# A fused two-block transformer on one core: context chain held for its conditioning, its weights loaded by SP, compressor loads two ahead, tail squares summed apart

## The chip, the cores and the metric

The kernel runs on one core of one Trainium2 chip. The metric is the device time of the whole program in microseconds (us). All of it is one launch; nothing is computed on the host but a relaying of the weights.

## The reference

The reference runs two blocks one after the other on x (512 tokens of width 1024). Cut to what matters here:

```
x = first_block(x, mem, ...)       # sparse attention + spatial gating, then x + memory_cross_attention(x, mem),
                                   # then x + relu(norm(x) @ w_ff1)^2 @ w_ff2           (d_ff = 4096)
for l in range(2):                 # second block, two layers; xc = ctx (256 tokens) is a second stream
    m  = silu(c)     @ w_mod[l] + b_mod[l]      # 9 rows of 1024: the conditioning of x
    mc = silu(c_ctx) @ w_mod[l] + b_mod[l]      # 9 rows of 1024: the conditioning of the context
    x  = ffn_sublayer(x, m, 0, ...);  xc = ffn_sublayer(xc, mc, 0, ...)
    h  = mod_norm(x, m, 1, ...);      hc = mod_norm(xc, mc, 1, ...)
    # layer 0: both streams are mixed (convolution, pooling, attention) and go through a second ffn_sublayer;
    # layer 1: the context only gives keys and values, kc and vc
return rms_norm_2(x, final_g)
# mod_norm(x, m, i, g) = rms_norm_2(x, g) * (1 + m[3i+1]) + m[3i];   a sublayer's result is gated by m[3i+2]
```

So `w_mod` (2 x 1024 x 9216, float32) is read once, and each of its 9 rows per layer is needed at a fixed place: rows 0 and 1 at a stream's first norm, row 2 at the gate of its first feed-forward part, rows 3 and 4 at its second norm, and so on.

## The kernel before, in words

**Streams and gemms.** x is kept transposed, 8 tiles of 128 x 512; memory and context are 8 tiles of 128 x 256. Products are float32 of high precision: a weight tile `raw` (128 x 1024, 512 KB) is loaded by SP, ScalarE rounds it (`whi`, line 356) and VectorE takes the rest (`wlo`, line 357), in halves; each product is three matmuls, hi by hi, hi by lo, lo by hi (lines 388 to 390 or 416 to 418). One weight tile of a 128-column output is thus 24 matmuls.

**`get`** (line 362) hands out the next weight tile in an order that a first dry pass recorded: it splits tiles up to two ahead (`ensure`), which loads raw tiles up to two further (three raw buffers), and then calls `tick`.

**Conditioning parts.** `tick` (line 565) advances the conditioning by one part (line 580): a tile `wm` (128 x 512, 256 KB, two buffers) is multiplied and summed on VectorE with silu(c), once for each stream that needs it (line 590: the result tile is called `wj` for a first stream and `wm` for the last), each followed by a short read of the sum into `modp`. `load_wm` (line 571) issues the loads, on ScalarE's queue, one part ahead. The plan has 336 parts: 48 for the context's rows 0 to 2 of layer 0, 48 for x's rows 0 to 2, 96 for rows 3 to 8 of both (two sums each), then layer 1. `need_mods` (line 606) runs the parts that are still missing at once, where a row is used.

**The chain of the context.** All work of the context in layer 0 is a generator, `ctx_chain` (line 1375): first norm, feed-forward part, second norm (`norm_c(0, 1)`), keys and values (`kv_c`, 8 weight tiles of 24 matmuls of 256 columns each), mixers, attention. It stands in a queue, and the main stream takes pieces of it where it expects TensorE to wait: `fill(ns)` draws pieces worth so many nominal ns; a piece that yields -1 ends the fill. So the chain runs during the sparse attention (`nsa`), then during the memory attention (line 1227), whose pipeline has 16 units (score product L1253, maximum L1255, exponential L1260, normalisation L1262, transposes L1271 two steps later, and per head a product with the values, L1281). With `norm_c(0, 1)` it asks for rows 3 and 4.

**Norms of x.** The eight squares of a norm are added up tile by tile (`sq_add`, line 451): the first adds on GpSimd, those after tile 3 on VectorE, each one tile late, and the last square is kept apart (`tail`). `col_rstd` (line 470) sums over the partitions with matmuls by ones: 4 blocks of 128 tokens, in each the sum and the tail; then VectorE scales, GpSimd takes the power, TensorE spreads the result over the partitions (L487).

**The compressor** (`compress`, line 906) of the sparse attention loads its own 8 weight tiles `fc` (512 KB) each right before its matmuls; `block1` calls a piece of it after each of the 16 steps of `project_uv`.

Of the kernel before, what the change touches and what calls it, by code (L numbers as in the profile page):

```python
# [206 lines left out]
class Squares:  # L207


    def __init__(self, ap):  # L210
        self.sum, self.tail = ap, None


class Order(list):
# [7 lines left out]
class Body:  # L222
# [137 lines left out]
    def get(self, key, tick=1, ahead=2, kept=False):  # L360
        i = len(self.used)
        self.used.append(key)
        if kept:
            self.used.kept.add(i)
        if self.order is None:
            _, _, nk, nc = self.pk.pieces[key]
            w = self.split_tiles(kept, nk * nc)
            for t in w:
                self.nc.gpsimd.memset(t.bitcast(F32), 0.0)
            self.tick(tick)  # L370
            return [t.rearrange("p (k n) -> p k n", k=nk) for t in w]
        assert self.order[i] == key, (self.order[i], key)
        self.ensure(i + ahead)
        self.tick(tick)
        w = self.split[i]
        self.split[i] = None
        return w
# [71 lines left out]
    def sq_add(self, ss, x, m, late=None, pool=False):  # L449


        if m == 0:
            self.nc.scalar.activation(ss.sum, x, AF.Square)
            return
        t = self.t2(x.shape[-1])
        self.nc.scalar.activation(t, x, AF.Square)
        on_vector = m > 3 and not pool and (late is not None or x.shape[-1] == T)
        add = lambda: (self.nc.vector if on_vector else self.nc.gpsimd).tensor_tensor(ss.sum, ss.sum, t, op=OP.add)
        if late is None or not on_vector:
            return add()  # L460
        if late:
            late.pop()()
        if m == 7:
            ss.tail = t
        else:
            late.append(add)

# [3 lines left out]
    def col_rstd(self, ss, n, dim, slow=False):  # L471

        nb = n // 128
        p = self.aux()
        parts = [ss.sum] + [ss.tail] * (ss.tail is not None)
        for b in range(nb):
            for i, t in enumerate(parts):
                self.nc.tensor.matmul(p[:, b:b + 1], t[:, b * 128:(b + 1) * 128], self.c("ones"), start=i == 0,
                                      stop=i == len(parts) - 1)
        return self.rstd(p[:, :nb], nb, 1.0 / dim, slow)  # L480

    def spread(self, y, nb, p=None, j0=0, step=1):

# [87 lines left out]
    def load_wm(self):  # L571

        while self.wm_loads < min(self.parts + 2, len(self.plan)):
            w = self.wp.tile([128, 512], F32, tag="wm", name="wm", bufs=2)
            l, j, half = self.plan[self.wm_loads][:3]
            self.nc.scalar.dma_start(w, self.d["wmod"][l, j, half])
            self.wms.append(w)
            self.wm_loads += 1

# [66 lines left out]
    def block1(self):  # L646
# [23 lines left out]
        with tc.tile_pool(name="b1", bufs=1) as self.b1:  # L670
            with tc.tile_pool(name="mix1", bufs=1) as mp:
# [33 lines left out]
                for i in range(2):  # L705
# [7 lines left out]
                    for h in range(2):  # L713
                        src = z[64 * h:64 * h + 64].rearrange("p (n t) -> p t n", t=16)
                        for par in range(2):
                            for q in range(2):
                                o = ksp[i][64 * par:64 * par + 64, 8 * q:8 * q + 8, 31 * h:31 * h + 31]
                                s = src[:, par::2, q:q + 31]
                                if par == 0:
                                    nc.scalar.copy(o, s)  # L720
                                else:
                                    nc.vector.tensor_copy(o, s)
                self.project_vg(hh, hl, v2, gates, pair)
                comp = self.compress(ksp, w2, kc, vc, rows, gg)
                memkv = self.mem_kv(mem, mss)
                mh, ml = self.new_h()
                yc = self.keep(2)
# [3 lines left out]
                for n, _ in enumerate(self.project_uv(hh, hl, u, vv, pair)):  # L731
# [8 lines left out]
                        next(memkv)  # L740
                    if n > 7:
                        next(ln, None)
                for g in (comp, ln, pre):
                    self.run(g)
                sg = self.spatial(u, vv, sgw, mh, ml)
# [159 lines left out]

    def compress(self, ksp, w2, kc, vc, rows, gg):
        nc = self.nc
        for i in range(2):
            ps = [self.aux(), self.aux()]
            for q in range(4):  # L910
                w1 = self.fc(F32)
                nc.sync.dma_start(w1, self.d["cw1"][i, q])
                for mt in range(2):
                    for j in range(4):
                        nc.tensor.matmul(ps[mt][:, :63], w1[:, j, mt * 128:(mt + 1) * 128], ksp[i][:, 4 * q + j],
                                         start=q == 0 and j == 0, stop=q == 3 and j == 3)
                yield 1700
            bias = self.small(2)
            ht = self.tc_(64), self.tc_(64)
# [368 lines left out]
    def ffn1(self, hh, hl, ss):  # L1288
        nc, x = self.nc, self.x
        with self.tc.tile_pool(name="ffn1", bufs=2) as fp:  # L1290
# [25 lines left out]
            def dn(g):  # L1316
                gh, gl = G.pop(g)
                late = []
                for mp_ in range(4):
                    w = self.get(("f2", g, mp_))  # L1320
                    for s in range(2):
                        m = 2 * mp_ + s
                        p = self.mm()
# [24 lines left out]
    def ctx_chain(self, y):  # L1348
# [2 lines left out]
        yield from self.norm_c(0, 0, y=y)  # L1351
        yield from self.ffn2(0, 0, False, True)
        self.ffn_ready = True
        yield from self.norm_c(0, 1)
        self.kc, self.vc = self.fc(F32), self.fc(F32)
        yield from self.kv_c(0, self.kc, self.vc)
# [419 lines left out]
    def mix_out(self, l, s, n, x, ss, mh, ml):  # L1776
# [2 lines left out]
        late = None if s else []  # L1779
        for m in range(8):  # L1780
            p = self.mm()[:, :n]
            self.gemm_fm([(p, mh, ml)], self.get((("o", l), m), s == 0))
            nc.vector.scalar_tensor_tensor(x[:, m], p, gate[:, m:m + 1], x[:, m], op0=OP.mult, op1=OP.add)
            self.sq_add(ss, x[:, m], m, late)
            if s == 0:
# [161 lines left out]
```

## Time and profile before

| | us |
|---|---|
| median of 3 runs (3606.37 to 3608.75) | 3607.94 |
| the profiled execution | 3608.67 |
| its span | 3606.9 |
| TensorE busy (PE) | 3363.2, 93% |
| VectorE busy (DVE) | 2045.1, 57% |
| ScalarE busy (ACT) | 1212.0, 34% |
| GpSimd busy (POOL) | 103.3, 3% |
| DMA, mean over the span | 110 GB/s |

PE is the engine to look at: it is busy nearly everywhere, so what matters is the few places where it is not, and which wait ends last there. The profiled execution took 1.8 us more than its span; that much lies around the instructions.

### The profile page before, as it was taken

The numbers are of one execution on the slowest core, as the hardware profiler recorded it, in microseconds if no ns is written. First come the engines' busy times: TensorE is split into PE (matmuls) and PEld (weight loads), VectorE is DVE, ScalarE is ACT, GpSimd is POOL, SyncE is SP. The second block draws the span as 40 slices with busy tenths as digits, with TensorE's granted clock in tenths as the row PEclk, the third lists the DMA queues.
The fourth block names the chain that finished last, engine by engine and source line by source line (L and its number), as shares of the span: only waits on it lengthen the run. The fifth ranks groups of instructions, "written<-read, shape, count | busy, mean of one in ns | idle before, by whom it ended". The sixth has DMA issues, their size and how long they took to land.

```text
span 3606.9 us, 48216 instructions
## 1 busy us (share of the span) xinstructions
PE 3363.2 (93%) x18878; PEld 2935.1 (81%) x18878; DVE 2045.1 (57%) x4231; ACT 1212.0 (34%) x2417; POOL 103.3 (3%) x156
## 2 busy tenths in 40 slices
PE   8969995089999999999999999999999999999999
PEld 7969985068887888788888888888888888878887
DVE  6578665657777766666564444463333454554445
ACT  6335542053333322236542221232122224633222
POOL 1100000010000000000000000010000010000000
PEclk9989997589999999999999999999999999999999
DMA  5444344425443544444333233212212113323332
GB/s 200 168 140 139 119 133 125 136 83 151 147 146 114 154 144 144 130 138 135 107 100 97 91 97 94 74 47 71 65 65 65 60 58 120 99 69 102 98 98 78
DMA packets 143348, 396.79 MB, mean 110 GB/s; under 512 B 16144, under 2 KB 27280, under 8 KB 142608
## 3 DMA queue, kind: packets, MB, share of 16 engines
q1 hardware_dynamic: 94736, 305.61, 26.7%
q10 hardware_dynamic: 48384, 88.10, 8.4%
q8 instruction: 148, 2.42, 0.3%
q14 instruction: 80, 0.66, 0.1%
HBM read 387.36 MB, written 2.10 MB: 108 GB/s over the span
## 4 chain that ended last, share of the span: by engine, by line
PE 83%; DVE 7%; DMA 4%; issue 3%; ACT 3%; POOL 1%; SPq 0%; ACTq 0%; DVEq 0%; POOLq 0%
PE mm L388 19%; PE mm L389 19%; PE mm L390 19%; PE aux L388 5%; PE aux L389 5%; PE aux L390 5%; DMA wm<-in_wmod 3%; DVE wlo L357 1%; PE aux L1748 1%; DVE wm L590 1%; PE mm L416 1%; PE mm L418 1%; PE mm L417 1%; PE mm L401 1%; PE mm L402 1%
## 5 line engine op out<-in xcount | busy, mean ns | idle before, releaser
L357 DVE TENSOR_TENSOR wlo<-raw,whi 128x512 fp32r<-128x512 f32 (+1 forms) x1060 | 692.7, 696 | 452.9 <-ACT whi L356 445.6
L388 PE MATMUL mm<-h,whi 128*128 128x512 f32 (+1 forms) x2352 | 898.3, 382 | 11.1 <-ACT whi L356 10.8
L356 ACT CAST whi<-raw 128x512 fp32r<-128x512 f32 (+1 forms) x1060 | 599.3, 616 | 906.1 <-issue 634.4
L389 PE MATMUL mm<-h,whi 128*128 128x512 f32 (+1 forms) x2352 | 894.3, 380 | 6.4 <-DVE h L512 5.8
L390 PE MATMUL mm<-h,wlo 128*128 128x512 f32 (+1 forms) x2352 | 891.4, 379 | 0.4 <-DVE wlo L357 0.4
L388 PEld LDWEIGHTS mm<-h,whi 128*128 128x128 f32 x2352 | 446.1, 190 | 93.5 <-ACT whi L356 11.0
L389 PEld LDWEIGHTS mm<-h,whi 128*128 128x128 f32 x2352 | 446.2, 190 | 87.7 <-DVE h L512 7.4
L390 PEld LDWEIGHTS mm<-h,wlo 128*128 128x128 f32 x2352 | 445.8, 190 | 83.8 <-DVE wlo L357 0.8
L388 PE MATMUL aux<-h,whi 128*128 128x256 f32 x1056 | 304.1, 288 | 0.7 <-DVE t L509 0.5
L389 PE MATMUL aux<-h,whi 128*128 128x256 f32 x1056 | 301.6, 286 | 0.5 <-DVE h L512 0.3
L390 PE MATMUL aux<-h,wlo 128*128 128x256 f32 x1056 | 301.3, 285 | 0.0
L388 PE MATMUL mm<-g,whi 128*128 128x512 f32 (+1 forms) x720 | 277.9, 386 | 0.0
L389 PE MATMUL mm<-g,whi 128*128 128x512 f32 (+1 forms) x720 | 277.7, 386 | 0.0
L390 PE MATMUL mm<-g,wlo 128*128 128x512 f32 (+1 forms) x720 | 276.7, 384 | 0.0
L590 DVE CUSTOM_DVE_ANT_0 wm<-wm,silu_c 128x512 f32<-128x512 f32 x336 | 232.0, 691 | 67.2 <-DMA wm<-in_wmod 61.0
L1400 DVE SCALAR_TENSOR_TENSOR x<-mm,gate,x 128x512 f32<-128x512 f32 x160 | 120.0, 750 | 180.4 <-PE mm L390 180.3
L388 PEld LDWEIGHTS aux<-h,whi 128*128 128x128 f32 x1056 | 205.0, 194 | 4.9 <-DVE t L509 0.9
L389 PEld LDWEIGHTS aux<-h,whi 128*128 128x128 f32 x1056 | 204.6, 194 | 4.8 <-DVE h L512 1.3
L390 PEld LDWEIGHTS aux<-h,wlo 128*128 128x128 f32 x1056 | 204.6, 194 | 0.0
L421 ACT CAST g<-t 128x512 fp32r<-128x512 f32 x88 | 54.6, 621 | 397.2 <-DVE t L1446 397.2
L1446 DVE SCALAR_TENSOR_TENSOR t<-t,mm 128x512 f32<-128x512 f32 x88 | 60.5, 688 | 212.8 <-PE mm L390 212.4
L390 PEld LDWEIGHTS mm<-g,wlo 128*128 128x128 f32 x720 | 135.3, 188 | 27.5
(364 smaller groups left out, 4898.0 us busy)
## 6 DMA issues: line engine op xcount, KB each, us to landing
raw<-in_w_a SPq DMA_DIRECT2D x220, 512.0 KB, 3.5
wm<-in_wmod ACTq DMA_DIRECT2D x336, 256.0 KB, 2.7
raw<-in_w_d SPq DMA_DIRECT2D x110, 512.0 KB, 3.5
raw<-in_w_in SPq DMA_DIRECT2D x84, 512.0 KB, 3.6
raw<-in_w_f SPq DMA_DIRECT2D x64, 512.0 KB, 3.5
raw<-in_w_out SPq DMA_DIRECT2D x32, 512.0 KB, 3.6
bias<-in_bias SPq DMA_DIRECT2D x64, 128.0 KB, 2.1
raw<-in_w_kv SPq DMA_DIRECT2D x8, 512.0 KB, 4.2
```

Source lines behind the costliest of these rows:

```text
L356: self.nc.scalar.copy(hi[:, cs], raw[:, cs])
L357: self.nc.vector.tensor_tensor(lo[:, cs], raw[:, cs], hi[:, cs].bitcast(F32), op=OP.subtract)
L388: mmul(o, wh[:, k, cols], h[:, k], start=s, stop=False)
L389: mmul(o, wh[:, k, cols], l[:, k], start=False, stop=False)
L390: mmul(o, wl[:, k, cols], h[:, k], start=False, stop=e)
L401: mmul(o, wh[:, k], h[:, k], start=n == 0, stop=False)
L402: mmul(o, wl[:, k], h[:, k], start=False, stop=False)
L416: mmul(o, h[:, k0 + k], wh[:, k], start=s, stop=False)
L421: self.nc.scalar.copy(hi, src)
L590: nc.vector.tensor_tensor_reduce(o, w, self.sc[:, s, ks], 1.0, 0.0, OP.mult, OP.add, wm[:, half, s, j % 8:j % 8 + 1])
L1400: nc.vector.scalar_tensor_tensor(xs, o, gate[:, m:m + 1], xs, op0=OP.mult, op1=OP.add)
L1446: nc.vector.scalar_tensor_tensor(hid, hid, 0.5, b, op0=OP.mult, op1=OP.mult)
```

## The change

There are five edits. `ctx_chain` yields -1 until the context's conditioning has been made up to row 4, before it starts its second norm. `load_wm` issues on SP's queue instead of ScalarE's, and `get` calls it ahead of the splits and raw loads. `block1` calls `tick` after every second step of `project_uv`; on the other side, the last weight tiles ahead of two kinds of norm (`f2` of the last group, `o` from tile 6) no longer tick. `compress` loads two tiles at its start, which is now ahead of `project_vg`, and one more after each of its pieces. `sq_add` keeps the last two squares out of the running sum, and `col_rstd` sums everything but the last square first, and the last one by itself into another PSUM tile.

```diff
-        self.sum, self.tail = ap, None
+        self.sum, self.tail = ap, []
...
         assert self.order[i] == key, (self.order[i], key)
+        if tick:
+            self.load_wm()
         self.ensure(i + ahead)
         self.tick(tick)
...
-        if m == 7:
-            ss.tail = t
+        if m > 5:
+            ss.tail.append(t)
...
-        parts = [ss.sum] + [ss.tail] * (ss.tail is not None)
+        if ss.tail:
+            v = self.small(nb)
+            self.token_sums(p, [ss.sum] + ss.tail[:-1], nb)
+            self.nc.vector.tensor_scalar(v, p[:, :nb], 1.0 / dim, EPS, op0=OP.mult, op1=OP.add)
+            p = self.aux()
+            self.token_sums(p, ss.tail[-1:], nb)
+            self.nc.vector.scalar_tensor_tensor(v, p[:, :nb], 1.0 / dim, v, op0=OP.mult, op1=OP.add)
+            return self.rsqrt(v, nb, slow)
+        self.token_sums(p, [ss.sum], nb)
+        return self.rstd(p[:, :nb], nb, 1.0 / dim, slow)
+
+    def token_sums(self, p, parts, nb):
         for b in range(nb):
             for i, t in enumerate(parts):
                 self.nc.tensor.matmul(p[:, b:b + 1], t[:, b * 128:(b + 1) * 128], self.c("ones"), start=i == 0,
                                       stop=i == len(parts) - 1)
...
-            self.nc.scalar.dma_start(w, self.d["wmod"][l, j, half])
+            self.nc.sync.dma_start(w, self.d["wmod"][l, j, half])
...
+                comp = self.compress(ksp, w2, kc, vc, rows, gg)
+                next(comp)
                 self.project_vg(hh, hl, v2, gates, pair)
-                comp = self.compress(ksp, w2, kc, vc, rows, gg)
...
+                    if n % 2:
+                        self.tick()
...
+        def load():
+            if todo:
+                ws.append(self.fc(F32))
+                nc.sync.dma_start(ws[-1], self.d["cw1"][todo.pop(0)])
+        load()
+        load()
+        yield 0
...
-                w1 = self.fc(F32)
-                nc.sync.dma_start(w1, self.d["cw1"][i, q])
+                w1 = ws.pop(0)
...
+                load()
                 yield 1700
...
-                    w = self.get(("f2", g, mp_))
+                    w = self.get(("f2", g, mp_), g < 7 or mp_ < 2)
...
         self.ffn_ready = True
+        while self.mods_done[1] < 5:
+            yield -1
         yield from self.norm_c(0, 1)
...
-            self.gemm_fm([(p, mh, ml)], self.get((("o", l), m), s == 0))
+            self.gemm_fm([(p, mh, ml)], self.get((("o", l), m), s == 0 and m < 6))
```

The first place where instructions move is VectorE's order in the memory attention, behind the last residual of the context's first feed-forward part (`xc`, L1412 before, L1439 now). Before, then now:

```order
L1412 SCALAR_TENSOR_TENSOR xc<-aux,gate,xc 128x256
L458 TENSOR_TENSOR ss<-ss,t_6429 128x256
L590 ISA wm,modp<-wm,silu_c 128x512
L590 ISA modp 128x1
...
L590 ISA wj,modp<-wm,silu_c 128x512
L590 ISA modp 128x1
L590 ISA wm,modp<-wm,silu_c 128x512
```

```order
L1439 SCALAR_TENSOR_TENSOR xc<-aux,gate,xc 128x256
L1308 TENSOR_TENSOR h<-aux,h 128x512
L1280 TENSOR_REDUCE sm<-mm 128x1
L1282 TENSOR_SCALAR sm<-sm,mr 128x1
L1286 RECIPROCAL sm<-sm 128x1
L1287 TENSOR_SCALAR t_6457<-t_6457,sm 128x256
```

Before, 100 sums of conditioning stand in a row there (36 parts for one stream, 32 for both), with the rest of the attention behind them; now the attention's next unit follows at once. Nowhere in VectorE's order now do more than 4 such sums stand in a row; before, there are two longer runs, this one and one of 7 at the start of the sparse attention.

The second place is TensorE's order in the same attention, from the transposes (L1271 before, L1296 now) of the unit in which the chain stops. Before, then now:

```order
L1271 MATMUL mm<-cst,t_6808 128x128 x2
L1253 MATMUL mm<-mk,mq 128x256
L388 MATMUL mm<-h,whi 128x256
L389 MATMUL mm<-h,whi 128x256
L390 MATMUL mm<-h,wlo 128x256
```

```order
L1296 MATMUL mm<-cst,t_6499 128x128 x2
L1278 MATMUL mm<-mk,mq 128x256
L1296 MATMUL mm<-cst,t_6519 128x128 x2
L1278 MATMUL mm<-mk,mq 128x256
L1296 MATMUL mm<-cst,t_6533 128x128 x2
L1278 MATMUL mm<-mk,mq 128x256
```

The context's 8 tiles of keys and values (192 matmuls of 256 columns), which stood between the attention's last units, are gone from here. They now stand in layer 0's mixing part, as pieces that `mix2` draws.

The third place is SP's order while the last tiles of the first projections are loaded (`in_w_in` 128x560 are `project_vg`'s weights, `in_cw` the compressor's). Before, then now:

```order
L338 DMA raw<-in_w_in 128x560 x4
L338 DMA raw<-in_w_in 128x1024 x2
L338 DMA raw<-in_w_kv 128x1024 x2
L338 DMA raw<-in_w_in 128x1024
L912 DMA fc<-in_cw 128x1024 x4
```

```order
L588 DMA wm<-in_wmod 128x512
L338 DMA raw<-in_w_in 128x560
L929 DMA fc<-in_cw 128x1024 x2
L588 DMA wm<-in_wmod 128x512
L338 DMA raw<-in_w_in 128x1024
L588 DMA wm<-in_wmod 128x512
L338 DMA raw<-in_w_in 128x1024
```

Nearly every raw tile now has a conditioning tile ahead of it on SP's queue, and the compressor's first two tiles are issued ahead of the next five raw tiles instead of behind them.

## Rows read from the trace of the kernel before

**Rows 1.** The page: busy tenths and granted TensorE clock in 40 slices.
```profile
PE   8969995089999999999999999999999999999999
...
PEclk9989997589999999999999999999999999999999
```

**Rows 2.** Waits of PE: who for whom, total us, times, longest.
```profile
PE mm L1271 <- DVE t L1262: 130.4, 2, 130.1
PE aux L985 <- DVE uv L986: 13.4, 3, 12.4
...
PE aux L478 <- DVE ss L458: 7.4, 4, 3.2
PE aux L915 <- DMA fc<-in_cw: 6.2, 2, 4.1
```

**Rows 3.** Stretches: length, busy per engine, PEclk, DMA share, GB/s.
```profile
60.00:120.00 60.00, 54.26 (x425) 52.90 (x424) 35.15 (x94) 32.46 (x67) 1.52 (x3) 0.91 0.59 197
186.45:199.03 12.58, 1.99 (x15) 1.58 (x13) 6.12 (x22) 0.00 (x0) 0.00 (x0) 0.72 0.51 141
594.84:724.44 129.60, 2.04 (x15) 1.49 (x13) 72.16 (x214) 1.26 (x3) 0.00 (x0) 0.51 0.48 138
724.44:774.22 49.78, 40.25 (x245) 34.60 (x246) 30.49 (x78) 26.66 (x67) 0.90 (x2) 0.86 0.29 94
800.00:1150.00 350.00, 349.35 (x1536) 288.92 (x1537) 251.19 (x521) 119.70 (x207) 8.36 (x6) 0.99 0.47 144
1530.00:1710.00 180.00, 174.63 (x1090) 157.00 (x1091) 121.94 (x261) 89.19 (x179) 1.39 (x25) 0.98 0.44 133
```

**Rows 4.** Chain of waits, 594 to 729 us: start, us, what.
```profile
594.84 2.65 DMA wm<-in_wmod
...
719.52 2.62 DMA wm<-in_wmod
722.17 0.69 DVE wj L590
722.91 0.69 DVE wm L590
...
725.03 0.34 DVE sm L1255
...
726.95 0.34 DVE sm L1255
...
728.87 0.34 DVE sm L1255
```

**Rows 5.** PE in order of time, one stretch of context weights.
```profile
759.15 0.28 PE L417 MATMUL mm<-wlo,h 128*128 128x256 f32 x1
...
764.66 0.28 PE L418 MATMUL mm<-whi,h 128*128 128x256 f32 x1
```

**Rows 6.** PE groups by form, 724.44 to 774.22: count, busy us, mean ns.
```profile
L1281 PE MATMUL aux<-mpt,mv 128*128 128x512 f32 x12 | 5.8, 610 | 1.4 <-ACT mpt L1272 1.4
```

**Rows 7.** Norm ahead of layer 0, VectorE in order of time.
```profile
1152.12 0.69 DVE L590 CUSTOM_DVE_ANT_0 wj<-wm,silu_c 128x512 bf16<-128x512 f32 x1
...
1155.09 0.68 DVE L1325 TENSOR_TENSOR x<-mm,x 128x512 f32<-128x512 f32 x1
...
1158.77 0.16 DVE L446 TENSOR_SCALAR sm<-aux 128x4 f32<-128x4 f32 x1 [2.32 <-PE aux L478]
```

**Rows 8.** The same norm and the next, PE in order of time.
```profile
1156.43 0.38 PE L478 MATMUL aux<-cst,ss 128*128 128x1 f32 x2 [3.24 <-DVE ss L458]
...
1526.82 0.38 PE L478 MATMUL aux<-cst,ss 128*128 128x1 f32 x2 [1.72 <-DVE ss L458]
```

**Rows 9.** DMA issues: KB each, median us to landing.
```profile
wm<-in_wmod ACTq DMA_DIRECT2D x336, 256.0 KB, 2.7
...
raw<-in_w_f SPq DMA_DIRECT2D x64, 512.0 KB, 3.5
```

**Rows 10.** Waits of SP's queue, 780 to 1150 us.
```profile
SPq L338 <- DVE wlo L357: 343.2, 66, 12.5
```

More of the change, by code (lines that the diff above doesn't have):

```diff
@@ L479, in col_rstd @@
                                       stop=i == len(parts) - 1)
-        return self.rstd(p[:, :nb], nb, 1.0 / dim, slow)
     def spread(self, y, nb, p=None, j0=0, step=1):
@@ L907, in compress @@
         nc = self.nc
+        todo = [(i, q) for i in range(2) for q in range(4)]
+        ws = []
+        def load():
[5 more added lines that the diff above has]
+        yield 0
         for i in range(2):
```

## The prediction

> **What bounds the kernel now.** I read the page's slices first [rows 1]. PE stands at 9 tenths or more nearly everywhere, so the kernel is bound by TensorE, and a change can only win where PE is not busy. Four such places are large enough to matter: the start, the third slice (6 tenths), and above all the seventh and eighth (5 and 0). A slice is 90 us; in the eighth PE does nothing at all, and the granted clock there is half.
>
> The waits of PE say who ends these gaps [rows 2]. One wait of 130.1 us for VectorE's normalisation in the memory attention is by far the largest; one of 12.4 us comes at the start of the sparse attention; the norms of x (L478, matmuls by ones that wait for the running sum of squares) lose 7.4 us in four waits, the compressor's loads 6.2 us in two.
>
> The chain of waits through the large gap shows what VectorE did instead of the normalisation [rows 4]. From 594.84 it alternates between a load of a conditioning tile (2.65 us) and a sum on it (0.69 us), later two sums, up to 723.6. That is `need_mods`: the context's second norm asks for rows 3 and 4 when 60 of the 128 parts they need are made, and the other 68 are made at once, each waiting for its own load because only two buffers exist. The stretches confirm it [rows 3]: in 129.60 us VectorE ran 214 instructions, PE 2.04 us. The stretch at 186.45 is the same thing in small, 7 parts before the chain's first norm, 12.58 us with PE at 1.99.
>
> **The change part by part.** All sums are made against the profiled execution, 3608.67 us (span 3606.9 and 1.8 around it), which is 0.7 above the median of 3607.94.
>
> *The hold, memory attention: 179.4 us become about 29.* Without the run of parts the attention's next unit follows at once. From 594.84 to the first matmul behind the attention, at 774.22, the kernel before takes 129.60 + 49.78 = 179.4 us [rows 3]. The changed kernel does the rest of the attention alone in that place, since the chain yields -1 and nothing else is queued. Ten units are left. Right behind the run, before the context's norm gets in between, units follow each other at 725.03, 726.95 and 728.87 [rows 4], so 1.92 us each, a loop of VectorE and ScalarE that PE does not bound: 19.2 us. Two heads end among them, and their products with the values stand ahead of the next score product on PE: 5.8 us for 3 heads [rows 6], so 1.9 each, 3.8 in all. The last unit then drains through transposes, a copy, one more such product and a copy, which I put at 3.4. That is 26.4. PE is mostly idle there, and the first stretch after the run shows a granted clock of 0.86 [rows 3], so some of these products and the first gemm run at 1.2 GHz; I add 2.6 and take 29. Ends: 24 if everything overlaps well, 40 if each unit takes 3 us, which is what 40 over 13 pipeline steps would be. Term: -150.4 (-155 to -139).
>
> TensorE: Matmul & The Clock Gate, section Part 1, in the Trainium skill says that an idle PE falls to 1.2 GHz and comes back only after sustained work. The trace agrees for the run itself (0.51). If PE stayed at the low level through the whole unfilled attention, the three products would cost twice 5.8 us, an estimate of 32 instead of 29 for this place; that lies within the ends above.
>
> *What had filled those 49.78 us moves, and is paid elsewhere: +20.5.* The context's keys and values are 8 tiles of 24 matmuls. In one undisturbed stretch 46 matmuls start in 764.66 - 759.15 = 5.51 us [rows 5], 0.12 each, so 192 of them are 23.0 us of PE. They now stand in layer 0's mixing part, where PE is busy 174.63 of 180 us [rows 3]. At most the 5.4 us of idle there can take them in: +17.6; at worst all of it plus some waits for their weight splits: +26. VectorE (121.94) and ScalarE (89.19 of 180) have room for the splits, so I take +20.5. The context's second norm now overlaps x's norm of the mixing part, a place where PE waits for VectorE; a first piece of it, two or three VectorE instructions, lies between x's: 0 to +4, I take +1.5.
>
> *The displaced parts themselves cost nothing.* The 100 sums (about 70 us of VectorE) go to the ticks of later weight tiles. In the feed-forward part of block 1 VectorE is busy 251.19 of 350 us with PE at 349.35 [rows 3]; it already makes one part per tile there, and the number per tile stays the same. The surplus only lengthens the list: it ends later, in layer 1's first feed-forward part, and no use comes before its part is made, by the order of ticks. If VectorE did fall behind, PE would wait at each residual; the order shows at most 4 sums in a row, 2.8 us, against 5.5 us of PE per tile (350 us for 1536 matmuls, so 64 tiles).
>
> *The extra ticks in the first projections: -10.* They bring 8 parts forward, so the run of 7 goes. The 12.58 us stretch [rows 3] shrinks to what the attention needs anyway; the sums, 8 x 0.69 = 5.5 us, go under gemms that bound there. Bounds: 0 if VectorE's backlog behind it ends last anyway, -12.6.
>
> *The compressor: -4.* Its loads take part in a stretch where PE is idle 5.7 of 60 us, and PE's two waits for them are 6.2 us [rows 2, 3]. Two tiles ahead covers a landing time of 3.5 us for 512 KB [rows 9]. But it is a chain through ScalarE and VectorE too, and another wait may come last: 0 to -6.
>
> *The norms: -8.* In `col_rstd` before, 4 blocks of two summands run from 1156.43 until VectorE's scaling at 1158.77 [rows 7, 8], 0.29 us a summand at mixed clock, 0.22 at the full one. Now the four of the sum go first, while the last square is still being made, and four remain: -0.9 us in five norms of x, -0.45 in the two halves of the last. In the norm ahead of layer 0 two more things go: VectorE still makes conditioning sums at 1152.12 and only then, at 1155.09, adds the last residual [rows 7]; without the ticks of the last two tiles it can do so at about 1153.3, where the gemm ends, so 1.8 more. 2.7 + 4.5 + 0.9 = 8. Bounds: -2 (the added instruction on VectorE and another PSUM tile eat it up) and -11. PE's waits there, 3.24 and 1.72 us [rows 8], leave room for it.
>
> *The loads on SP: 0.* They hold up nothing on ScalarE any more, and ScalarE was not the bound. On SP each now waits for the sum made one tick earlier, and the raw tile behind it waits along. In block 1's feed-forward part SP already waits 343.2 of 370 us for VectorE's splits [rows 10], so it runs as far ahead as its buffers let it; the sum follows the split directly, 0.7 or 1.4 us later. A raw tile is asked for two tiles (11 us) before its split is due and lands in 3.5 us. Where tiles follow faster, in the first 300 us, this could cost something: the ends are -8 (the loads of the sparse attention's ticks leave earlier than behind ScalarE's work) and +12.
>
> Sum: -150.4 + 20.5 + 1.5 - 10 - 4 - 8 = -150.4. 3608.67 - 150.4 = 3458.3, and less the 0.7 to the median 3457.5; I say 3457.
>
> **The rivals.** *SP's queue becomes the bound at the start.* It carries 197 GB/s in the stretch from 60 us [rows 3], and now loads, each with a wait for VectorE in front, are interleaved with the projections' weights. If some 16 tiles each come 1 to 1.5 us late, that is +16 to +24: about 3477. Against it: raw tiles run four tiles ahead. Chance 0.12.
>
> *The gain is larger.* The attention alone takes 24, the context's tiles find all the idle time of the mixing part (+17.6), the sparse attention wins from earlier loads (-8): 3458 - 5 - 3 - 8, about 3441. Chance 0.2.
>
> *The unfilled attention runs long.* Each unit at 3 us and the products at the low clock: 45 instead of 29, 3473. For it: in the kernel before, the filled units took longer than 1.92 us; against it: the filling was the reason. Chance 0.13.
>
> *Slower than before: the loads on one queue go one after the other.* A raw tile takes 3.5 us to land and a conditioning tile 2.7 [rows 9]. If they did not overlap any more, a tick would need 6.2 us of queue per weight tile, against 5.5 us of PE. That would add 0.7 us to each of some 280 ticked tiles, +200 us, which outweighs the hold: about 3655. It decides from 0.55 us per tile on. Against it: these are times to landing, not occupation; in 800 to 1150 us 144 GB/s go at a DMA share of 0.47, and 197 GB/s went at the start [rows 3]. Chance 0.03.
>
> DMA: Bandwidth & Descriptors, section Queues, rings and completion order, in the Trainium skill says that each DMA engine takes turns between the queues that have work, and takes one queue's descriptors in ring order. A conditioning tile issued behind a raw tile thus loses its turn and lands later; no run here shows by how much yet. Its section Issuing engines are not separate DMA queues says that issuing from several engines saves only issue time. By both, the throughput stays, and the rival just named keeps its small chance.
>
> *The change doesn't do what it says*: another run of parts forms at a later use, and time stays near 3600. The order shows none longer than 4 sums. Chance 0.02.
>
> **How the numbers follow.** The forecast has 0.5, the rivals 0.12, 0.2, 0.13, 0.03 and 0.02. With the likeliest case alone the range would be 3444 to 3470, from the uncertainty of the moved tiles and the attention. It reaches to the larger gain and to the two costs: 3432 to 3487; the ends of all terms together (3433 and 3509) meet only if every one of them falls on the same side. About 0.2 per cent, 7 us, is what a measurement of this kernel can tell from no change. Faster 0.95, same 0.02, slower 0.03.
>
> **What would show it.** The slices must lose the 0 and the 5 beside it; the wait of 130 us must be gone, and the attention from its sixth unit to the first gemm must take 24 to 40 us. PE's busy time must stay near 3363 us, since no gemm is removed. The mixing part of layer 0 must be some 20 us longer between the same two norms. VectorE's waits for conditioning tiles must be a few us. The prediction is wrong if PE shows new waits for `whi` or `wlo` that end in a raw load behind a conditioning load, if a run of sums stands anywhere before a norm, or if the first 300 us do not shrink.

## The result, and the profile after

The changed kernel takes 3470.3 us (median; 3464.65 to 3476.67) against 3608.35 us of the kernel before, run beside it: ratio 0.9618, 95% interval 0.9599 to 0.9638. The forecast was 3457, its range 3432 to 3487. Run again (e9 below) it was 3468.7 against 3608.9. The profiled execution took 3467.17 us, 141.5 less than that of before, where the sum had 150.4.

The page's slices of the kernel after, busy tenths of PE and its granted clock, answer to [rows 1]:
```profile
PE   9989998999999999999999999999999999999999
PEclk9999998999999999999999999999999999999999
```
The 0 and the 5 are gone, and no slice's clock is at half any more. PE's waits, to be read beside [rows 2]:
```profile
PE mm L1296 <- DVE t L1287: 12.1, 8, 2.8
PE mm L390 <- ACT whi L356: 11.6, 2, 8.3
PE aux L499 <- POOL sm L431: 8.9, 4, 4.6
PE aux L1161 <- DVE t L1145: 7.2, 4, 2.1
...
PE aux L1010 <- DVE uv L1011: 1.0, 2, 0.7
...
PE aux L491 <- DVE ss L460: 0.6, 1, 0.6
PE aux L939 <- DMA fc<-in_cw: 0.5, 1, 0.5
```
(L1296 was L1271, L1010 was L985, L491 was L478, L939 was L915.) The 130.4 us are 12.1 in eight short waits, the 13.4 of the sparse attention are 1.0, the compressor's 6.2 are 0.5, and the norms' 7.4 on VectorE's sum are 0.6.

Where the 141.5 us come from is read by laying the same instruction of both traces side by side: the context's last residual in the memory attention (594.26 before, 570.14 after), the second matmul of the gemm behind it (774.28, 601.06), and the power on GpSimd in each norm of x.

| stretch | forecast | measured |
|---|---|---|
| start to the context's last residual | -14 | -24.1 |
| memory attention from there to the gemm | -150.4 | -149.1 |
| gemms and feed-forward up to the norm ahead of layer 0 | -2.7 | -2.9 |
| layer 0's first feed-forward and norm | -0.9 | +0.2 |
| layer 0's mixing part, with the context's norm and tiles | +22 | +29.5 |
| the rest, four norms and the end | -4.4 | +4.9 |

The memory attention and layer 0's mixing part as stretches (us; PE busy, PEld, VectorE, ScalarE, POOL; granted clock; DMA share; GB/s), first of before between those points, then of after:
```profile
594.26:774.28 180.02, 42.94 (x261) 36.37 (x260) 103.23 (x293) 28.16 (x72) 0.90 (x2) 0.61 0.43 125
1533.80:1815.00 281.20, 276.60 (x1731) 244.35 (x1732) 179.21 (x397) 141.57 (x307) 5.15 (x27) 0.99 0.42 125
```
```profile
570.14:601.06 30.92, 18.38 (x58) 9.73 (x57) 13.10 (x45) 12.03 (x38) 0.00 (x0) 0.83 0.00 0
1357.40:1668.56 311.16, 305.84 (x1933) 273.21 (x1934) 202.00 (x447) 156.12 (x339) 5.13 (x27) 0.98 0.39 124
```
In the first, PE's work falls from 261 matmuls to 58, and 149.1 us go. In the second, 202 matmuls and 29.2 us of PE come; the idle time there is 5.3 us after and was 4.6 before, so none of it took the moved tiles in.

ScalarE's exponentials in the memory attention, one a unit, in order of time, show what is left there:
```profile
573.13 0.56 ACT L1285 ACTIVATE t<-mm,sm,mr 128x256 f32<-128x256 f32 x1 [1.34 <-DVE sm L1282]
...
575.04 0.56 ACT L1285 ACTIVATE t<-mm,sm,mr 128x256 f32<-128x256 f32 x1 [1.00 <-DVE sm L1282]
...
578.75 0.56 ACT L1285 ACTIVATE t<-mm,sm,mr 128x256 f32<-128x256 f32 x1 [0.94 <-DVE sm L1282]
...
583.24 0.56 ACT L1285 ACTIVATE t<-mm,sm,mr 128x256 f32<-128x256 f32 x1 [1.40 <-DVE sm L1282]
```
Units inside a head follow each other at 1.9 us, as read from [rows 4]. Where PE's product of a finished head with the values stands between two units (it is issued two steps behind the head's last unit), it is 4.5 us, here from 578.75 to 583.24, and the chain of waits (start, us, what) goes through that product and two copies:
```profile
578.94 2.29 PE aux L1306 x4
581.25 0.59 ACT h L1307
581.87 0.69 DVE h L1308
```
The product is slow, and the granted clock is low there: 0.78 from 578.94 to 581.25, 0.77 around the next product (589.12 to 591.46), 0.59 around the last (597.64 to 601.06). Its group by form in the changed kernel:
```profile
L1306 PE MATMUL aux<-mpt,mv 128*128 128x512 f32 x14 | 9.4, 801 | 0.5 <-ACT mpt L1297 0.5
```
It takes 801 ns each against 610 in [rows 6], where the clock was 0.86 [rows 3].

### The profile page after: what moved, and what is told of

It reads as the page before. It is cut to its first block, busy times and chain, and to the rows that moved or that the text cites. A ratio compares the mean times of both kernels' runs of the same rounds, so it can differ in the third digit from the quotient of the medians.

```text
span 3465.5 us, 48468 instructions
## 1 busy us (share of the span) xinstructions
PE 3369.6 (97%) x18938; PEld 2940.2 (85%) x18938; DVE 2035.5 (59%) x4231; ACT 1210.7 (35%) x2417; POOL 105.1 (3%) x156
## 4 chain that ended last, share of the span: by engine, by line
PE 85%; DVE 6%; ACT 3%; issue 3%; DMA 1%; POOL 1%; SPq 0%; POOLq 0%; ACTq 0%; DVEq 0%
PE mm L390 20%; PE mm L391 19%; PE mm L392 19%; PE aux L390 5%; PE aux L392 5%; PE aux L391 5%; DVE wlo L357 2%; PE aux L1775 1%; PE mm L418 1%; PE mm L420 1%; PE mm L419 1%; PE mm L403 1%; PE mm L404 1%; PE mm L408 1%; PE aux L1161 1%
```

## The experiments

Each run stands beside runs of the kernel before on its chip. "Spatial gate" is the start of the power on GpSimd in that norm: 257.2 us before, 233.6 after. The profile shows one execution; in the profiles of other runs that are the same up to there it lies at 232.8 to 235.7.

**The hold alone, and all but the hold**

```diff
 # e1: the kernel before, with only
         self.ffn_ready = True
+        while self.mods_done[1] < 5:
+            yield -1
```


> The kernel before with the hold alone: the chain yields -1 until rows 3 and 4 of its conditioning are made; loads, ticks, compressor and norms as before. Theory (the hold is the change, the other edits win the first 240 us): memory attention from its sixth unit to the first gemm 31 to 32 us instead of 179.4, layer 0's mixing part about 29 us longer, the norm of the spatial gate at 257 us as before and not at 234: 3608 - 149 + 29 + 2 = about 3490, ratio 0.967. Rival (the other edits win nothing of their own, the first 240 us only moved time forward): about 3470, ratio 0.962.

Measured: 3493.8 us, ratio 0.9684 (0.9669 to 0.9700). The start is as before (spatial gate at 253.4), and layer 0's mixing part, from norm to norm, is as long as in the changed kernel:
```profile
1380.96:1696.18 315.22, 307.44 (x1939) 274.25 (x1939) 206.40 (x458) 156.88 (x340) 7.01 (x30) 0.97 0.40 125
```
That is 29.3 more than the 285.95 of before. The theory held; the rival's 3470 is 24 us away.

```diff
 # e12: the changed kernel without the hold
         self.ffn_ready = True
-        while self.mods_done[1] < 5:
-            yield -1
```


> The changed kernel without the hold: the context's second norm asks for its rows in the middle of the memory attention again, and about 68 parts are made at once, their loads now issued by SP. Theory (hold and other edits add: 114 for the hold alone, 139 for all): 25 us less than before, about 3583, with one wait of PE of 120 to 135 us. Rival (loads on SP run ahead of the sums better than ScalarE's, the run of parts gets short by itself): a wait under 100 us and 3550 or less.

Measured: 3586.1 us, ratio 0.9931 (0.9914 to 0.9948). PE's wait in the memory attention is back, loads on SP or not:
```profile
PE mm L1296 <- DVE t L1287: 128.5, 2, 127.7
```
The hold alone wins 113.6, all the rest alone 24.5; together 138.1, and the whole change 138.1. Within the noise the two add; each ratio is known to some 6 us either way, so that the sum comes out to a tenth is chance.

**The start: compressor, loads, ticks**

```diff
 # e3: the compressor as before
+                self.project_vg(hh, hl, v2, gates, pair)
                 comp = self.compress(ksp, w2, kc, vc, rows, gg)
-                next(comp)
-                self.project_vg(hh, hl, v2, gates, pair)
 ...
-                w1 = ws.pop(0)
+                w1 = self.fc(F32)
+                nc.sync.dma_start(w1, self.d["cw1"][i, q])
```


> The changed kernel with the compressor's loads as before (one tile, asked for when it is used, started behind the gates' projection). Theory (two ahead pays at the start): the stretch from the layer normalisation to the norm of the spatial gate, 95.4 us now and 107.2 before, grows by 6 to 12 us, 3476 to 3482. Rival (that stretch was shortened by the conditioning loads leaving SP instead of ScalarE): grows by under 3 us, 3470 to 3473.

```diff
 # e4: ScalarE issues the conditioning loads again, at the tick
-            self.nc.sync.dma_start(w, self.d["wmod"][l, j, half])
+            self.nc.scalar.dma_start(w, self.d["wmod"][l, j, half])
 ...
-        if tick:
-            self.load_wm()
```


> The changed kernel with the conditioning weights issued by ScalarE again, at the tick as before. Theory (loads on SP cost and bring nothing): 3470 within 4, the norm of the spatial gate within 2 us of 233.6. Rival (loads behind ScalarE's work were late in the first 300 us): 5 to 12 us longer there, 3475 to 3482. A second rival (conditioning loads delay the raw tiles on SP): shorter by 3 us or more.

The third is e3 and e4 together:

> The changed kernel with both the compressor's loads and ScalarE's issue of the conditioning loads as before. Undoing the first alone gave 3496, the second alone 3481. Theory (the two are one edit: loads on SP stand in the way of the compressor's unless these go ahead): less than their sum of +37, and less than the first alone, 3480 to 3490. Rival (each pays on its own): 3500 to 3510.

| median us (spatial gate at) | loads on ScalarE | loads on SP |
|---|---|---|
| compressor as before | e7: 3495.4 (253.2) | e3: 3496.1 (259.4) |
| compressor two ahead | e4: 3481.2 (245.3) | changed: 3470.3 (233.6) |

The ratios are 0.9692 (0.9679 to 0.9705) for e7, 0.9694 (0.9679 to 0.9709) for e3, 0.9654 (0.9637 to 0.9671) for e4. Taking back the compressor costs 26 us, more than the theory's 6 to 12, and not where it was expected: the stretch from the layer normalisation to the spatial gate did not grow (95.0 us for 95.4); the loss lies ahead of it, between the second and third norm. Taking back SP's loads costs 11, so in e4 the theory (loads on SP bring nothing) fell and the first rival held: 3481.2 lies in its 3475 to 3482, and the spatial gate comes 11.7 us later. For e7 both ranges were missed. That the two losses do not add to 37 is shown; that both together cost less than the first alone is not (3495.4 and 3496.1 are the same within the noise). With the old compressor it makes no difference who issues the loads. They are one edit in two parts. The chain of waits of e3 says why:
```profile
142.33 4.82 DMA wm<-in_wmod
...
149.22 0.69 DVE wm L602
149.95 0.33 SPq L588
150.33 4.50 DMA fc<-in_cw
```
A compressor load that is asked for when it is used stands in SP's queue behind a conditioning load, and that one waits for a sum on VectorE. PE waits 18.9 us in three such places (0.5 after), and the clock falls with it, from 0.97 over the 52.22 us between the second and third norm to 0.86 over 70.80:
```profile
PE aux L929 <- DMA fc<-in_cw: 18.9, 3, 8.7
```
```profile
93.58:164.38 70.80, 59.76 (x447) 59.22 (x447) 31.72 (x91) 20.92 (x48) 4.45 (x7) 0.86 0.52 176
```
In e4 the queue is ScalarE's. Its chain of waits, and below ScalarE's own waits from 80 to 170 us:
```profile
110.12 7.45 DMA wm<-in_wmod
117.59 0.69 DVE wm L600
118.39 0.32 ACT tc L945
118.76 0.85 PE aux L954 x8
```
```profile
ACT uv L915 <- DVE mod L607: 3.9, 1, 3.9
ACT uv L915 <- DVE modp L600: 3.5, 1, 3.5
```
ScalarE's work on u and v stands behind issues that wait for VectorE's sums (the changed kernel has no such row), the next load lands late, and VectorE's sum on it keeps the compressor's small operation behind it waiting. PE loses 7.3 us in that one place, and its next matmuls follow at 0.21 us instead of 0.12 (granted clock 0.54 from 118.76 to 124.40). DMA: Bandwidth & Descriptors, section Issuing engines are not separate DMA queues, in the Trainium skill says that another issuing engine saves only issue time. With the old compressor the times agree with it (3495.4 and 3496.1), and a conditioning load takes the same time from issue to landing from either queue, 2.6 us (median) on SP's and 2.7 on ScalarE's. The 11 us come from what an issue waits for and what stands behind it, in instruction order.

```diff
 # e5: no ticks in u and v
-                    if n % 2:
-                        self.tick()
```


> The changed kernel without the ticks in the first projections (every second piece of u and v), all else as in the changed kernel. Theory (they take the run of 7 forced parts away): the run is back ahead of the context's first norm, 8 to 13 us, about 3480, with the stretch from the layer normalisation to the spatial gate's norm at 103 to 108 us instead of 95.4. Rival (the loads of these ticks lie on SP between the projections' weights and the compressor's, and cost what they bring): the stretch between the second and third norm, 52 us now, becomes shorter by 5 us or more and the time stays at 3470 within 4.

Measured: 3478.3 us, ratio 0.9641 (0.9628 to 0.9654), spatial gate at 241.6: 8.0 us by the profile and 8.0 by the medians. The run of forced parts is back as one wait of PE:
```profile
PE aux L1008 <- DVE uv L1009: 13.2, 2, 12.5
```
The theory held. The ticks pay only with the loads, though: e7 has them and reaches the spatial gate at 253.2, e1 has none and does so at 253.4.

**The norms**

```diff
 # e6: one square kept apart, one sum, as before
-        if m > 5:
+        if m == 7:
             ss.tail.append(t)
 ...
-            self.token_sums(p, ss.tail[-1:], nb)
-            self.nc.vector.scalar_tensor_tensor(v, p[:, :nb], 1.0 / dim, v, op0=OP.mult, op1=OP.add)
```


> The changed kernel with the norms as before: one square kept apart, the sums of both in one PSUM tile, one scaling on VectorE. Theory (where PE has the context's products behind the norm, the four more summands only take PE time, and elsewhere they win what was forecast): from the last residual to the power on GpSimd 0.6 us shorter in the norms with the context's products beside them, 0.9 longer in the others, -1 to +2 in all: 3470 within 4. Rival (the forecast of 0.9 in five norms and 0.45 twice): 5.4 us more, about 3475.5.

Measured: 3470.2 us, ratio 0.9618 (0.9605 to 0.9631): no difference from the changed kernel. From the last residual on VectorE to the first gemm of x, in us:

| norm ahead of | before | changed | e6 |
|---|---|---|---|
| layer 0 | 8.66 | 7.55 | 8.31 |
| mixing 0 | 8.37 | 7.58 | 9.78 |
| layer 0's second feed-forward (context's mixers beside it) | 8.67 | 12.62 | 10.56 |
| layer 1 (context's products behind it) | 10.31 | 10.94 | 10.31 |
| mixing 1 (context's products behind it) | 10.07 | 12.46 | 10.07 |
| the last feed-forward | 9.14 | 6.68 | 8.70 |

The edit wins 0.8 to 2.2 us in three norms and loses 0.6 to 2.4 in the three where PE has other work. Over all six it wins nothing (55.2, 57.8 and 57.7 us), as the equal times say. PE in order of time at the norm ahead of mixing 1 shows the loss, before and then after:
```profile
2961.99 0.31 PE L478 MATMUL aux<-cst,ss 128*128 128x1 f32 x2
...
2963.50 0.36 PE L478 MATMUL aux<-cst,t 128*128 128x1 f32 x2
2967.40 1.05 PE L487 MATMUL aux<-cst,sm 128*128 128x128 f32 x8
2970.11 0.50 PE L401 MATMUL mm<-h,whi 128*128 128x512 f32 x1 [1.66 <-ACT h L510]
```
```profile
2820.21 0.28 PE L491 MATMUL aux<-cst,ss 128*128 128x1 f32 x2
...
2821.69 1.55 PE L491 MATMUL aux<-cst,t 128*128 128x1 f32 x10
2828.00 1.05 PE L499 MATMUL aux<-cst,sm 128*128 128x128 f32 x8
2830.72 0.50 PE L403 MATMUL mm<-h,whi 128*128 128x512 f32 x1 [1.66 <-ACT h L522]
```
16 passes by ones became 24, and what stands behind them comes later: from the first pass to the spread, 5.41 us became 7.79. Half of the 2.4 lost are the eight passes themselves (1.74 us from the first pass to the next matmul became 2.90). The other half is the clock, which was at its upper level behind the 16 passes and at its lower one behind the 24, with PE busy throughout (before, then after):
```profile
2963.73:2967.40 3.67, 3.67 (x33) 3.67 (x32) 2.10 (x5) 1.25 (x3) 3.09 (x4) 1.00 0.01 2
```
```profile
2823.11:2825.81 2.70, 2.70 (x13) 2.70 (x14) 0.65 (x2) 0.42 (x1) 1.02 (x1) 0.50 0.00 0
```

**The moved tiles, and versions that place them elsewhere**

```diff
 # e8: two ticks at each tile of the projection behind the sparse attention
-                self.gemm_fm_pair([([(p, mh, ml)], self.get(("out", m), 1, 2 - m)) for m, p in enumerate(ps)],
+                self.gemm_fm_pair([([(p, mh, ml)], self.get(("out", m), 2, 2 - m)) for m, p in enumerate(ps)],
 ...
-                    self.gemm_fm([(p, mh, ml)], self.get(("out", m)))
+                    self.gemm_fm([(p, mh, ml)], self.get(("out", m), 2))
```


> The changed kernel with two ticks instead of one at each of the 8 weight tiles of the projection behind the sparse attention, so that 130 parts are made at the norm ahead of layer 0 instead of 122 and the hold ends there: the context's second norm lies beside that norm and not beside the next, and its keys and values come one at a time into layer 0's mixing part. Theory (the mixing part's 29.5 us are 23 of PE and some 6 of waits and low clock, from five tiles in a row): 4 to 8 us less there, 0 to 2 more at the norm ahead of layer 0, 3463 to 3468. Rival (the tiles cost PE time wherever they stand, and the sums delay the residuals of the projection): 3470 to 3474.

Measured: 3470.0 us, ratio 0.9625 (0.9612 to 0.9638), no gain. The mixing part from norm to norm, without the context's norm and with the tiles spread out:
```profile
1354.94:1669.88 314.94, 307.20 (x1940) 274.07 (x1939) 202.90 (x447) 157.64 (x340) 6.16 (x29) 0.97 0.38 122
```
314.94 against 315.43 in the changed kernel: my theory that five tiles in a row cost waits fell. What the stretch does spend is PE time, 307.20 us of it; the account below says on what.

```diff
 # e2: the context's rows 3 and 4 earlier
-        self.plan = (half(0, (0, 3), 1, 2) + half(0, (0, 3), 0, 1) + half(0, (3, 9), 0, 2) + half(1, (0, 5), 0, 2)
+        self.plan = (half(0, (0, 5), 1, 2) + half(0, (0, 5), 0, 1) + half(0, (5, 9), 0, 2) + half(1, (0, 5), 0, 2)
 ...
-                    if self.parts < 48:
+                    if self.parts < 80:
                         self.tick()
```


> The changed kernel with the context's rows 3 and 4 of layer 0 made right behind its rows 0 to 2 (32 more sums in all, since x's rows 3 and 4 are now made apart), and the ticks of the context's feed-forward and of the sparse attention going on up to 80 parts instead of 48. The hold then ends before the memory attention, and the context's keys and values fill it again. Theory (the 29.5 us that the mixing part is longer are the price of the moved tiles, and the memory attention's waits take them in): memory attention 45 to 50 us instead of 31.5, mixing part back at 286: 3470 + 16 - 29 = about 3457. Rival (the sparse attention has no room on VectorE for more sums): 20 to 32 sums of 0.69 us come on top there, about 3475 or more.

Measured: 3481.9 us, ratio 0.9653 (0.9637 to 0.9668): the rival. The first stretch of the sparse attention, 47.95 us in the changed kernel with VectorE at 42.80, is 61.16 here; below it the memory attention's and the mixing part's stretches, from norm to norm:
```profile
253.22:314.38 61.16, 49.94 (x367) 46.15 (x367) 55.16 (x146) 25.88 (x64) 1.09 (x2) 0.94 0.59 204
536.68:679.48 142.80, 125.44 (x712) 106.43 (x711) 84.39 (x198) 74.28 (x154) 13.33 (x13) 0.93 0.29 95
1388.33:1680.09 291.76, 283.80 (x1745) 250.96 (x1746) 186.39 (x417) 142.21 (x308) 6.15 (x28) 0.97 0.35 117
```
The mixing part gets 23.7 us back and the memory attention takes 19.2: PE has 23.0 us more work there, and its idle time only falls from 21.2 to 17.4. Filling this attention, which waits for VectorE, hid little.

The last three ran on one chip. e10 has a tick at every piece of u and v and one square apart where the context's products follow; e11 is e10 with the plan of e2, the ticks for it put into the later units of the sparse attention:
```diff
 # e10
-                    if n % 2:
-                        self.tick()
+                    self.tick()
 ...
+            ss.one = with_c and not s
 ...
-        if m > 5:
+        if m > 5 + ss.one:
 # e11, besides the plan of e2
-                    if self.parts < 48:
+                    if self.parts < (48 if n < 24 else 76):
```


> The changed kernel once more, beside the two versions below on the same chip: 3470 within 6.

> The changed kernel with a tick at each piece of u and v (16 instead of 8), so that fewer sums fall into the sparse attention's first part, and with one square apart instead of two in the two norms that have the context's products beside them. Theory (the sparse attention's first 70 us are bound by VectorE, and there each of 8 sums costs its 0.69 us; the first 8 ticks won 8 us as their lack showed): 5 to 8 us less there, 3 less at the two norms, 3460 to 3463. Rival (with 16 ticks the loads on SP come in the way of the projections' weights): the 52 us between the second and third norm grow by what is won, 3467 to 3470, the 3 us of the norms alone.

> The kernel just above with the context's rows 3 and 4 of layer 0 made behind its rows 0 to 2, and the ticks that they need (28) in the sparse attention's later units, where PE is busy 80 of 80 us and VectorE 58: the hold is over before the memory attention, and the context's keys and values fill it. Theory (the earlier version of this lost 17 us to sums in the sparse attention's first part, and won 23.7 - 19.2 = 4.5 at the memory attention and the mixing part together): 4 to 5 us below the kernel just above, 3456 to 3458. Rival (sums cost there too, or the fuller memory attention takes back more): not below it.

Measured: e9 3468.7 us (0.9612, 0.9599 to 0.9625); e10 3469.9 (0.9615, 0.9602 to 0.9628); e11 3460.7 (0.9590, 0.9577 to 0.9603). In e10's profile the stretch from the layer normalisation to the spatial gate takes 90.39 us for the changed kernel's 95.41, as expected, but its time over the runs (3465.3 to 3474.0) is not lower. The median lies in the rival's range, but what the rival rests on, a longer stretch between the second and third norm, is not seen either (51.93 us). Neither is shown. e11 is the fastest version tried, 8.0 us below e9 by the medians, though the intervals still touch. In its profile:
```profile
246.99:456.40 209.41, 205.42 (x1681) 196.33 (x1680) 169.97 (x416) 111.40 (x258) 3.50 (x7) 1.00 0.50 160
519.91:665.28 145.37, 128.46 (x708) 110.09 (x708) 84.80 (x198) 74.36 (x154) 13.36 (x13) 0.91 0.29 93
1374.88:1666.78 291.90, 283.92 (x1745) 251.11 (x1746) 186.38 (x417) 142.28 (x308) 6.15 (x28) 0.97 0.36 117
```
The sparse attention takes 209.41 us for 58 more VectorE instructions (most of them the 28 displaced sums and their short reads), 207.31 without: where PE bounds, the sums are nearly free. Memory attention and mixing part together are 437.3 us against 439.1. These two differences cancel, so the profile does not show what the moved rows gain: e11's profiled execution, the slowest of its five (3464.6), is only 0.7 us below e10's (3465.3), while the medians differ by 9.2, more than the expected 4 to 5. Against e9's profile it is 4.0 us shorter, and 3.2 of these lie ahead of the spatial gate (235.34 in e9, 232.11), not where the moved rows are. Where the rest of the 8 us lies stays open.

## Why the prediction was right, and where its terms were off

**The hold.** Right in place, mechanism and size: 149.1 us against 150.4 went at that place. Its parts held too: ten units are left (573.13 to 595.36), they follow at 1.9 us against 1.92, a head's product adds 2.6 where I put 1.9, and from the last unit to the gemm it is 5.7 where drain and low clock had 6.0. By the rule on an idle PE's clock (the Trainium skill, TensorE: Matmul & The Clock Gate, Part 1) it would have been 32 for the forecast's 29. The same points give 30.3 (30.92 less the 0.6 by which my starting point lay later), at a clock of 0.83, between the two.

**The moved tiles: +20.5 and +1.5 became +29.5.** The tiles themselves cost what was put: their 192 matmuls stand between 1431.96 and 1478.60, and counted from start to start they take 23.0 us, 0.12 each. The step that failed is "at most the 5.4 us of idle there can take them in". None of it took them in (4.6 us of idle before, 5.3 after), and e8 showed that the order of the tiles is not why. That the idle places of a mixing part are waits within a chain, which a tile at another time does not fill, fits the unchanged waits but is argued.

That leaves some 6 us that are not the tiles' price. They are there with the old sums too (315.22 in e1, 315.17 in e6, from norm to norm), and without the tiles: e2, e11 and e12 have them elsewhere, and their mixing parts take 291.8, 291.9 and 291.0 us against 285.95 before. What these traces have in common is the clock, 0.97 to 0.98 over the stretch against 0.99 before. The forecast took it as unchanged. One spell at half clock of before (first line) became three in the changed kernel:
```profile
1529.91:1536.73 6.82, 5.01 (x15) 4.17 (x16) 4.36 (x7) 2.29 (x4) 0.16 (x1) 0.50 0.00 0
```
```profile
1354.77:1361.59 6.82, 5.22 (x16) 4.06 (x15) 5.62 (x9) 2.95 (x5) 0.58 (x2) 0.50 0.01 2
1504.95:1511.78 6.83, 6.30 (x29) 6.30 (x30) 4.14 (x9) 3.95 (x10) 0.00 (x0) 0.50 0.55 173
1665.38:1668.56 3.18, 3.18 (x17) 3.18 (x18) 0.43 (x3) 0.00 (x0) 0.00 (x0) 0.50 0.00 0
```
PE is busy for 14.7 us at half clock instead of 5.0, and as work at half clock takes twice as long, that is up to 4.8 of the 6 (an estimate). Why the clock falls at 1504.95 and not at the like place before stays open; with one trace of the kernel before, it may also be that this trace was a lucky one.

**The start: -14 became -24.1.** The ticks were sized well (-10 put, 8.0 in e5). The failed step is that compressor and loads were priced apart, -4 and 0: the runs show an interaction. Two ahead is worth 14 with ScalarE's loads (3495.4 to 3481.2) and 26 with SP's; SP's loads are worth 11 with the compressor two ahead and nothing without. The rival of SP's queue at the start, 3477, was a real danger: e3 is that mechanism, and the compressor's early loads are what keeps it off. That a conditioning tile on SP's queue lands later, as the prediction inferred, the rows do not show (2.6 us for 2.7, as above). The 3.5 us put for a load of the compressor was the row of another load; its own took 5.9 us (median) before.

**The norms: -8 became about -1.5.** The failed step is "-0.9 us in five norms". The sum by parts pays where PE idles, and costs PE time where it does not; I had treated all norms like the one of [rows 8]. Over the six norms of the table the sums win nothing. The ticks left out ahead of layer 0 won nearly what was put, 1.5 for 1.8: from norm to norm that feed-forward part takes 340.2 us in e6, which has the old sums, and took 341.7. As e6 has the other edits too, the 1.5 may in part be theirs.

**The rest: -4.4 became +4.9.** Of the 4.9 us, 2.4 are the norm ahead of mixing 1 and 0.6 the last norm, both from the sums by parts. Another 2.0 lie between x's norm ahead of layer 0's second feed-forward part and the context's behind it (41.5 to 43.5 us), nearly all in the first 10 us behind x's norm, where the granted clock is 0.65 and was 0.83. 1.2 lie at the context's norm in layer 1 (17.9 to 19.1): two sums of conditioning (at 2275.03 and 2275.64) stand there right ahead of the norm's scaling on VectorE, and none did before. Both are there with the hold alone (43.5 and 19.1 in e1), so they belong to the shifted order of the context's work. The norm ahead of the last feed-forward part gives 2.5 back.

So the displaced sums are not free everywhere: at that norm they stand in the way. In block 1's feed-forward part they cost nothing: PE is busy 336.63 of 336.63 us from 643.37 on, and was 335.90 of 336.71 from 817.29 on. The case of loads one after another did not come.

**The total.** That 3470.3 lies only 13 us from the forecast's 3457 is in part luck: the start brought 10 us more than was put, while the mixing part and the rest took 17 more. The mechanism of the largest term was right; the sizes of the small ones were not.

## What to carry to other kernels

Where a producer is pulled in by its consumer, look at what runs when it is late: one guard that lets the rest go on was worth 114 us here, four times all tuning beside it. Price edits that share an in-order queue together, not one by one; a load that waits for a buffer delays every load behind it, so those behind must be asked for early. Idle time of PE within a stretch is not room by itself: here none of 5 us took in work put beside it. When work is moved, look at the granted clock of the stretch too, before and after.

## What was not expected of the hardware

A sum over partitions by a matmul with ones of one column is not small: 16 passes of 128x1 take from 2961.99 to the next matmul's start at 2963.73, 0.11 us each, nearly as much as a pass over 256 columns (0.12). Nor does a busy PE keep its clock: behind 24 such passes the granted clock was 0.50 over 2.70 us with PE busy in all of them, and 256-column matmuls stood 0.21 us apart; behind 16 passes it was 1.00. Waits of up to 8.7 us also slow the work beside them: the same 447 matmuls between the second and third norm take 55.84 us of PE in e1, at a clock of 0.93, and 59.76 in e3, at 0.86. And the same program differs by up to 12.5 us from run to run (before: 3601.6 to 3614.1 on one chip), so that effects under 5 us were read from stretches of a trace, not from the time. Stretches of one trace vary as well (the spatial gate by 3 us), so what a single one shows to a microsecond is not more than that.
